# The low halves of the projection weights computed on VectorE instead of GpSimd

## The chip, the cores and the metric

The kernel runs on one core of one Trainium2 chip. A core has TensorE (PE, with its weight loads shown as PEld), VectorE (DVE), ScalarE (ACT), GpSimd (POOL) and SyncE (SP, which here only sends DMAs). Each takes its own instructions strictly in order. The metric is the time of one execution on the device in microseconds; of several runs the median is given.

## The reference

One layer of a hybrid decoder on 512 tokens of width 2048, in fp32:

```
xn   = rmsnorm(h, attn_norm_g)
proj = xn @ w_in                       # 2048 x 7184: columns of both head groups
o_a  = hgrn2(a_q, a_f, a_i)            # 8 heads, S_t = diag(f_t) S_{t-1} + (1-f_t) v_t
o_b  = gated_delta(l2norm(conv(q)), l2norm(conv(k)), conv(v), beta, g)   # 8 heads
h    = h + concat(gated_rmsnorm(o_a), gated_rmsnorm(o_b)) @ w_out
hn   = rmsnorm(h, ffn_norm_g)
qry  = hn @ w_query                    # 8 heads x 2 halves x 128
s1, s2 = qry[..., :128] . sub_keys[0], qry[..., 128:] . sub_keys[1]
best, pos = top16(top16(s1) + top16(s2)); gate = softmax(best)
h    = h + sum_e gate_e * gelu(hn . u_e) * v_e       # 16384 experts, 128 picked a token
out  = rmsnorm(h, final_norm_g)
```

## The kernel before, in words

**Two halves of a weight.** Every large product is made of three matmuls in a reduced fp32 format (fp32r). A weight block of 128 x 1024 (`wunit`, line 94) is loaded by SP into `wr`; ACT copies it to `wh` in that format (line 100, the high half); a subtraction `wl = wr - wh` makes the low half (line 102). The activations are split alike (`xh`, `xl`, later `yh`, `yl`, and `mh`, `ml` for the mixed heads). PE then adds `wh*xh + wh*xl + wl*xh` for each of the block's eight 128 x 128 pieces (`mm3`, lines 239 to 241; `linear`, lines 113 to 115; `scores`, lines 946 to 950, where the raw `wr` is used as well). The three tiles `wr`, `wh`, `wl` have three buffers each.

**Which engine subtracts.** `wunit` takes an engine. The expert tables (`u_steps`, `v_chunk`) ask for DVE: 512 blocks. The three projections do not, and get POOL: 114 blocks of the input projection, 32 of the output projection, 32 of the query projection, 178 in all.

**Stages.** (1) Prologue: load x, split it, sum its squares. POOL squares eight of the sixteen slices (line 774), DVE adds them up (line 776), and the sum gives the norm. (2) Four gated-delta pairs, each a chain of small steps: decays, keys, a block inverse by forward substitution on DVE (lines 498 and 500, 31 steps), a detour through DRAM (gNd, gTd), the rest of the inverse on PE (lines 527, 533, 542), then a recurrence over four chunks (lines 557 to 576). Between these steps the stream of input projections runs on PE: each step of the chain lets it go forward by a given rate (`run`, 1.8 pieces a step for the pairs, 5 for the HGRN heads). A finished projection goes through a causal convolution on DVE (lines 362 and 364) or a gate. Line 380 is the sum of squares for q's and k's norm. (3) Eight HGRN heads, first step line 614. (4) Output projection. (5) PEER scores: for each of 16 n a product, its scaling by the norm on DVE (`t_y`, line 956), four small score products (line 959) and top-16 steps on DVE; after each second n the sums `cd` (line 977) and their top-16. (6) All 16384 experts for 352 tokens, and the picked ones for 160 tokens by gathered rows.

**What sets the order.** The program is written as generators that yield to each other, and a scheduler then places each engine's instructions by a cost model and by the readiness of their inputs and buffers. The order on each engine is fixed when the program is built. So the engine of one instruction also moves others.

The lines that the change touches and what calls them:

Of the kernel before, what the change touches and what calls it, by code (L numbers as in the profile page):

```python
# [14 lines left out]
F32 = mybir.dt.float32  # L15
# [6 lines left out]
ALU = mybir.AluOpType  # L22
# [55 lines left out]
class Kernel:  # L78
# [12 lines left out]
        return (pool or self.fp).tile(list(shape), dt, tag=tag, name=self.nm(tag), bufs=bufs)  # L91


    def wunit(self, src, raw=False, eng=None):
        nc, wp = self.nc, self.wp
        full = raw
        raw = wp.tile([P, 8, P], F32, tag="wr", name=self.nm("wr"))
        nc.sync.dma_start(raw, src)
        hi = wp.tile([P, 8, P], F32R, tag="wh", name=self.nm("wh"))
        nc.scalar.copy(hi, raw)  # L100
        lo = wp.tile([P, 8, P], F32R, tag="wl", name=self.nm("wl"))
        (eng or nc.gpsimd).tensor_tensor(lo, raw, hi.bitcast(F32), op=ALU.subtract)  # L102
        return (raw, hi, lo) if full else (hi, lo)

    def linear(self, src, halves, xh, xl, ps):
# [1001 lines left out]
    def u_steps(self, et):  # L1107

        nc = self.nc
        ps = self.pt("lin")[:, 0:TD]  # L1110
        for h in (0, 1):
            hi, lo = self.wunit(self.a["u"][et][h], eng=nc.vector)
            for k in range(8):
                self.mm3(ps, hi[:, k], lo[:, k], 8 * h + k, k + h == 0, 8 * h + k == KT - 1)
            if h == 0:
                yield
        hid = self.ft("hid", (P, TD), bufs=2, pool=self.dp)
        nc.vector.tensor_tensor(hid, ps, self.r[:, 0:TD], op=ALU.mult)
        nc.scalar.activation(hid, hid, AF.Gelu)
        yield  # L1120
        yield hid
# [29 lines left out]
    def v_chunk(self, g, dc, w, last):  # L1151

        nc = self.nc
        wh, wl = w
        hi, lo = self.wunit(self.a["v"][g, dc].rearrange("p (x y) -> p x y", x=8), eng=nc.vector)
        hv, lv = (x.rearrange("p (e z) n -> p e (z n)", e=4) for x in (hi, lo))
        for dd in range(2):
            dt = 2 * dc + dd
            sl = slice(dd * P, (dd + 1) * P)
            ps = self.pt(self.vtags[self.vn % len(self.vtags)])[:, 0:TD]  # L1160
            self.vn += 1
            for e in range(4):
                nc.tensor.matmul(ps, hv[:, e, sl], wh[:, e], start=(e == 0), stop=False)  # L1163
                nc.tensor.matmul(ps, hv[:, e, sl], wl[:, e], start=False, stop=False)  # L1164
                nc.tensor.matmul(ps, lv[:, e, sl], wh[:, e], start=False, stop=(e == 3))  # L1165
            nc.vector.tensor_tensor(self.hT[:, dt], self.hT[:, dt], ps, op=ALU.add)
            if last:
                if dt == 0:
                    self.acc = self.ft("t_acc", (P, TD), pool=self.fop)
                self.square_sum(self.acc, [(self.hT[:, dt], slice(0, TD))], dt == 0, nc.vector)  # L1170
                nc.scalar.activation(self.hT[:, dt], self.hT[:, dt], AF.Copy, scale=self.g_fin[:, dt:dt + 1])
# [174 lines left out]
```

## Time and profile before

| | |
|---|---|
| three runs, median | 3533.93 us (3527.35 to 3548.31) |
| profiled execution, its own time | 3537.38 us |
| its span, first to last instruction | 3534.2 us |
| busy: PE, PEld, DVE, ACT, POOL | 94%, 87%, 78%, 34%, 25% of the span |
| mean granted clock of PE | 0.966 |
| POOL's subtractions (line 102) | 178, 432.8 us, starting from 6.8 to 1336.5 us |
| DVE's subtractions (line 102) | 512, 623.3 us, starting from 1347.2 us on |

Times are in microseconds; "x52" is a count of instructions. A row of a group gives line, engine, operation, out<-in, shapes and count, then busy time and the mean length of one in ns, then the idle time of the engine just before these instructions and what ended it. A row in order of time gives start, length, engine, line and, in brackets, a wait before it and what ended that. In a table of stretches each engine's busy time stands with its count, then PE's granted clock, the DMA engines' share and the rate in GB/s. Matmuls are pipelined: the length of one is more than its share of PE's time.

### The profile page before, as it was taken

To read this page: it belongs to the slowest core of one execution; us is meant where nothing else is said; L and a number is where in the kernel's file an instruction comes from. 1 tells how busy PE (TensorE), PEld (TensorE's weight loads), DVE (VectorE), ACT (ScalarE), POOL (GpSimd) and SP (SyncE) were. 2 spreads that over 40 slices of the span, in tenths; PEclk is the share of its full clock that TensorE was granted. 3 is DMA by queue.
4 is the path that set the end of the run, shared out by engine and by line. 5 is a ranking of instruction groups with operands and counts; after the bars stand their busy time and mean duration, and the time that the engine had idled before them with its cause. 6 is when DMAs were issued, how large, how long until landed. Compare 5 with 4: busy or idle time off the path is not lost.

```text
span 3534.2 us, 49832 instructions
## 1 busy us (share of the span) xinstructions
PE 3323.9 (94%) x19740; PEld 3085.3 (87%) x19740; DVE 2760.3 (78%) x4095; ACT 1206.8 (34%) x1499; POOL 878.8 (25%) x533
## 2 busy tenths in 40 slices
PE   7889899999999997898999799999999998999997
PEld 5667678888788896898989799999999998999997
DVE  7675654444534679998999799998999998999966
ACT  5333433322332212343435233332333334333334
POOL 4232223333354231011121222222222222111100
PEclk9899989999999998999999999999999999999999
DMA  4232222222442223677788899999999999999963
GB/s 147 76 96 88 83 64 81 78 81 78 130 130 85 71 66 120 209 293 292 277 318 294 316 346 375 370 368 355 358 360 365 372 366 333 349 322 335 332 183 111
DMA packets 238028, 801.63 MB, mean 227 GB/s; under 512 B 30202, under 2 KB 99066, under 8 KB 194978
## 3 DMA queue, kind: packets, MB, share of 16 engines
q1 hardware_dynamic: 191714, 462.88, 37.9%
q0 software_dynamic: 46080, 335.56, 25.2%
q8 instruction: 154, 2.52, 0.3%
q14 instruction: 80, 0.66, 0.1%
HBM read 754.50 MB, written 43.86 MB: 226 GB/s over the span
## 4 chain that ended last, share of the span: by engine, by line
PE 51%; DVE 19%; issue 14%; DMA 12%; POOL 2%; ACT 1%; SPq 0%; DVEq 0%; POOLq 0%; ACTq 0%
PE lin L239 8%; PE lin L241 7%; PE lin L240 7%; DMA row<-vn,eidx 3%; DVE wl L102 3%; DMA wr<-u 3%; PE g L1165 2%; PE g L1164 2%; PE g L1163 2%; POOL row L1205 2%; PE lin L1165 2%; PE lin L1164 2%; PE lin L1163 2%; DVE row L1218 2%; DMA wr<-v 1%
## 5 line engine op out<-in xcount | busy, mean ns | idle before, releaser
L100 ACT CAST wh<-wr 128x1024 fp32r<-128x1024 f32 x690 | 724.5, 1050 | 1708.8 <-DMA wr<-v 402.3
L241 PE MATMUL lin<-yh,wl 128*128 128x352 f32 x2048 | 673.0, 329 | 68.5 <-DVE wl L102 68.2
L102 DVE TENSOR_TENSOR wl<-wr,wh 128x1024 fp32r<-128x1024 f32 x512 | 623.3, 1219 | 81.6 <-ACT wh L100 80.3
L239 PE MATMUL lin<-yh,wh 128*128 128x352 f32 x2048 | 673.3, 329 | 9.5 <-ACT wh L100 9.5
L240 PE MATMUL lin<-yl,wh 128*128 128x352 f32 x2048 | 668.0, 326 | 0.0
L102 POOL TENSOR_TENSOR wl<-wr,wh 128x1024 fp32r<-128x1024 f32 x178 | 432.8, 2432 | 872.8 <-ACT wh L100 809.8
L241 PEld LDWEIGHTS lin<-yh,wl 128*128 128x128 f32 x2048 | 391.3, 191 | 78.8 <-DVE wl L102 78.4
L1205 POOL DMA_INDIRECT row<-un,eidx x160 | 212.4, 1328 | 809.7 <-DVE row L1218 626.2
L239 PEld LDWEIGHTS lin<-yh,wh 128*128 128x128 f32 x2048 | 391.7, 191 | 11.3 <-ACT wh L100 11.3
L1205 POOL DMA_INDIRECT row<-vn,eidx x160 | 201.2, 1258 | 782.8 <-DVE y_nat L1231 416.0
L240 PEld LDWEIGHTS lin<-yl,wh 128*128 128x128 f32 x2048 | 391.1, 191 | 0.0
L239 PE MATMUL lin<-xh,wh 128*128 128x512 f32 x912 | 381.4, 418 | 8.9 <-ACT xh L766 8.8
L1165 PE MATMUL g<-wgh,wl 128*128 128x352 f32 x1188 | 384.9, 324 | 3.5 <-DVE wl L102 3.3
L1164 PE MATMUL g<-wgl,wh 128*128 128x352 f32 x1188 | 385.4, 324 | 0.0
L1163 PE MATMUL g<-wgh,wh 128*128 128x352 f32 x1188 | 382.4, 322 | 2.3 <-ACT wh L100 2.3
L240 PE MATMUL lin<-xl,wh 128*128 128x512 f32 x912 | 375.5, 412 | 2.5 <-DVE xl L767 2.3
L241 PE MATMUL lin<-xh,wl 128*128 128x512 f32 x912 | 373.0, 409 | 4.4 <-POOL wl L102 4.4
L1231 DVE SCALAR_TENSOR_TENSOR y_nat<-row,ww,y_nat 128x2048 f32<-128x2048 f32 x128 | 300.3, 2346 | 11.1 <-DMA row<-vn,eidx 10.7
L1218 DVE SCALAR_TENSOR_TENSOR row<-row,hn_nat 128x2048 f32<-128x2048 f32 x128 | 292.1, 2284 | 1.7 <-DMA row<-un,eidx 1.5
L1165 PEld LDWEIGHTS g<-wgh,wl 128*128 128x128 f32 x1188 | 223.3, 188 | 5.5 <-DVE wl L102 5.4
L1163 PEld LDWEIGHTS g<-wgh,wh 128*128 128x128 f32 x1188 | 223.5, 188 | 2.6 <-ACT wh L100 2.6
L1164 PEld LDWEIGHTS g<-wgl,wh 128*128 128x128 f32 x1188 | 223.2, 188 | 0.0
(348 smaller groups left out, 5879.5 us busy)
## 6 DMA issues: line engine op xcount, KB each, us to landing
wr<-u SPq DMA_DIRECT2D x256, 512.0 KB, 6.2
wr<-v SPq DMA_DIRECT2D x256, 512.0 KB, 6.7
wr<-wi SPq DMA_DIRECT2D x114, 512.0 KB, 3.6
gd<-st SPq DMA_DIRECT2D x11, 2048.0 KB, 13.6
gm<-gd SPq DMA_DIRECT2D x32, 704.0 KB, 9.3
wr<-wo SPq DMA_DIRECT2D x32, 512.0 KB, 3.6
wr<-wq SPq DMA_DIRECT2D x32, 512.0 KB, 3.5
hidd<-hid SPq DMA_DIRECT2D x64, 176.0 KB, 5.2
```

Source lines behind the costliest of these rows:

```text
L100: nc.scalar.copy(hi, raw)
L102: (eng or nc.gpsimd).tensor_tensor(lo, raw, hi.bitcast(F32), op=ALU.subtract)
L239: mm(ps, hi, self.xh[:, k], start=first, stop=False)
L240: mm(ps, hi, self.xl[:, k], start=False, stop=False)
L241: mm(ps, lo, self.xh[:, k], start=False, stop=last)
L1163: nc.tensor.matmul(ps, hv[:, e, sl], wh[:, e], start=(e == 0), stop=False)
L1164: nc.tensor.matmul(ps, hv[:, e, sl], wl[:, e], start=False, stop=False)
L1165: nc.tensor.matmul(ps, lv[:, e, sl], wh[:, e], start=False, stop=(e == 3))
L1205: ins = nc.gpsimd.indirect_dma_start(out=r, out_offset=None, in_=self.a[tab], in_offset=bass.IndirectOffsetOnAxis(ap=idx, axis=0))
L1218: nc.vector.scalar_tensor_tensor(r, r, 1.0, hn, op0=ALU.mult, op1=ALU.mult, accum_out=ww[:, i:i + 1])
L1231: nc.vector.scalar_tensor_tensor(y, r, ww[:, i:i + 1], y, op0=ALU.mult, op1=ALU.add)
```

## The change

`wunit` loses its engine argument and always subtracts on DVE. The calls that named DVE drop the argument. Nothing else is edited; POOL keeps the eight squares of the prologue, a memset, small scalings in the output projection, a copy, five of the final products, and all gathers.

```diff
-    def wunit(self, src, raw=False, eng=None):
+    def wunit(self, src, raw=False):
...
         hi = wp.tile([P, 8, P], F32R, tag="wh", name=self.nm("wh"))
         nc.scalar.copy(hi, raw)
         lo = wp.tile([P, 8, P], F32R, tag="wl", name=self.nm("wl"))
-        (eng or nc.gpsimd).tensor_tensor(lo, raw, hi.bitcast(F32), op=ALU.subtract)
+        nc.vector.tensor_tensor(lo, raw, hi.bitcast(F32), op=ALU.subtract)
...
-            hi, lo = self.wunit(self.a["u"][et][h], eng=nc.vector)
+            hi, lo = self.wunit(self.a["u"][et][h])
...
-        hi, lo = self.wunit(self.a["v"][g, dc].rearrange("p (x y) -> p x y", x=8), eng=nc.vector)
+        hi, lo = self.wunit(self.a["v"][g, dc].rearrange("p (x y) -> p x y", x=8))
```

The scheduler orders the first five stages anew; from the end of the scores on, every engine has the same order as before. Three places show it. The names carry running numbers that are the same in both programs.

On PE, at the first step of the inverse of the first pair (L527; `lin` is the projection that runs beside it), before:

```order
L240 MATMUL lin_1049<-xl,wh_1098 128x512
L241 MATMUL lin_1049<-xh,wl_1100 128x512
L239 MATMUL lin_1049<-xh,wh_1098 128x512
L527 MATMUL g_814<-fc,gT 32x32 x8
L240 MATMUL lin_1049<-xl,wh_1098 128x512
L241 MATMUL lin_1049<-xh,wl_1100 128x512
```

and now:

```order
L239 MATMUL lin_1179<-xh,wh_1235 128x512
L240 MATMUL lin_1179<-xl,wh_1235 128x512
L527 MATMUL g_814<-fc,gT 32x32 x8
L241 MATMUL lin_1179<-xh,wl_1237 128x512
L239 MATMUL lin_1179<-xh,wh_1235 128x512
```

The same step of the chain has the next projection beside it: 416 projection matmuls stand ahead of it instead of 364. At the first step of the first HGRN head (L614) it is 1512 instead of 1423; at the second head's the counts are 1586 and 1584, and from there on equal.

On DVE, near the end of the first pair's substitution (L498, L500), before:

```order
L498 TENSOR_TENSOR t_sq_721<-iN_531,iT_532 128x8x6
L500 TENSOR_TENSOR iT_532<-iT_532,t_sq_721 128x8x6
L498 TENSOR_TENSOR t_sq_724<-iN_531,iT_532 128x8x5
L500 TENSOR_TENSOR iT_532<-iT_532,t_sq_724 128x8x5
L498 TENSOR_TENSOR t_sq_727<-iN_531,iT_532 128x8x4
```

and now:

```order
L498 TENSOR_TENSOR t_sq_721<-iN_531,iT_532 128x8x6
L444 TENSOR_TENSOR geg_389<-gq_507,geg_389 128x512
L500 TENSOR_TENSOR iT_532<-iT_532,t_sq_721 128x8x6
L444 TENSOR_TENSOR geg_410<-gq_507,geg_410 128x512
L498 TENSOR_TENSOR t_sq_724<-iN_531,iT_532 128x8x5
L102 TENSOR_TENSOR wl_1237<-wr_1233,wh_1235 128x1024
L500 TENSOR_TENSOR iT_532<-iT_532,t_sq_724 128x8x5
```

A subtraction stands between two steps of the substitution, and q's scaling (L444) has come forward.

On DVE, in the scores, around the scaling of a product whose predecessor closes a pair of n (L956), now:

```order
L968 MATCH_REPLACE c_1457_8661<-best,cd_8660 128x256
L956 TENSOR_TENSOR t_y_8745<-lin_8668,rstd 128x512
L969 MAX best<-c_1457_8661 128x8
L102 TENSOR_TENSOR wl_8778<-wr_8774,wh_8776 128x1024
L970 MAX_INDEX pos<-best,c_1457_8661 128x8
L966 MAX v_8076<-g_8747 128x8
L102 TENSOR_TENSOR wl_8816<-wr_8812,wh_8814 128x1024
```

Before, these rows stood there without the two subtractions. On PE nine matmuls of the next product (lin_8773) came ahead of the score products of this one (L959) before; now two do, because the third reads wl_8778:

```order
L946 MATMUL lin_8773<-yh,wh_8776 128x352
L947 MATMUL lin_8773<-yl,wh_8776 128x352
L959 MATMUL g_8747<-skt,t_y_8745 128x128 x4
L948 MATMUL lin_8773<-yh,wl_8778 128x352
L950 MATMUL lin_8773<-xg,wr_8774 128x160
```

On SP, the write of the first pair's substitution (gTd, L504) stands behind two more weight loads than before (wr_1378 and wr_1442), and its reading back (gT, L508) behind two more as well (wr_1442 and wr_1472).

## The prediction

> **What bounds the kernel now.** I read the page first (engines, slices; the granted clock is the one slice row that matters below), then busy time by stage, then who waits for whom in the stages that the change touches, then the rows in order of time on VectorE (DVE) and GpSimd (POOL).
>
> ```profile
> PEclk9899989999999998999999999999999999999999
> ```
>
> Not one engine bounds this kernel from end to end, so I cut it at its stages: prologue, gated-delta pairs, HGRN heads, output projection, PEER scores, and the expert part.
>
> ```profile
> core 0: us, PE busy (x) PEld busy (x) DVE busy (x) ACT busy (x) POOL busy (x), PEclk, DMA share, GB/s
> 0.00:60.00 60.00, 39.39 (x127) 27.47 (x127) 48.66 (x62) 32.84 (x45) 33.26 (x21) 0.91 0.47 170
> 60.00:514.00 454.00, 404.44 (x2058) 315.96 (x2058) 287.63 (x579) 171.62 (x236) 127.71 (x52) 0.87 0.28 84
> 514.00:930.00 416.00, 412.66 (x2252) 342.45 (x2251) 191.60 (x363) 122.07 (x145) 137.52 (x58) 1.00 0.25 78
> 930.00:1113.00 183.00, 178.36 (x795) 146.31 (x795) 71.35 (x84) 65.02 (x101) 87.83 (x47) 1.00 0.41 127
> 1113.00:1353.00 240.00, 223.97 (x1457) 219.34 (x1455) 165.41 (x760) 43.23 (x50) 72.93 (x32) 0.97 0.24 75
> 1353.00:3534.00 2181.00, 2065.05 (x13060) 2033.79 (x13058) 1995.65 (x2250) 772.05 (x924) 419.57 (x325) 0.98 0.85 311
> ```
>
> After 1353 us the subtraction is already on DVE and the order of every engine is the same in both kernels; those 2181 us I leave alone. The HGRN heads and the output projection keep TensorE (PE) busy 99% and 97% of the time at full clock with DVE under half: PE sets their length, and no term comes from them. What can move lies in the prologue, the pairs and the scores.
>
> How much is in the pairs? One full stretch gives the price of a 512-wide projection matmul, and one row per stage gives their number (one of three equal lines).
>
> ```profile
> 1000.00:1100.00 100.00, 100.00 (x443) 82.81 (x442) 33.86 (x36) 29.23 (x46) 52.04 (x28) 1.00 0.30 96
> 60.00:514.00 454.00, 172.49 (x408) 81.85 (x408) 0.87 0.28 84
> 514.00:930.00 416.00, 190.15 (x464) 87.30 (x464) 1.00 0.25 78
> ```
>
> 100/443 is 0.226 us a matmul. The HGRN stage has 3 x 464 = 1392 of them, 314 us; its other 860 matmuls have at most 416 - 314 = 102 us, 0.12 us each. By these prices the pairs' 1224 + 834 matmuls need at most 277 + 100 = 377 of their 454 us. So at least 77 us of PE time there go to waits and to the lower clock (0.87), about 19 us for each of the four pairs. The longest named wait:
>
> ```profile
> PE g L380 <- ACT t_sq L376: 30.2, 4, 9.1
> PE g L959 <- DVE t_y L956: 15.8, 7, 2.4
> ```
>
> The first row is the pairs', the second the scores'. Both waits end with DVE work, so DVE's delays count in these two stages.
>
> **The change part by part.** 178 subtractions leave POOL and come to DVE (114 units of the input projection, 32 of the output projection, 32 of the query projection).
>
> ```profile
> L102 DVE TENSOR_TENSOR wl<-wr,wh 128x1024 fp32r<-128x1024 f32 x512 | 623.3, 1219 | 81.6 <-ACT wh L100 80.3
> L102 POOL TENSOR_TENSOR wl<-wr,wh 128x1024 fp32r<-128x1024 f32 x178 | 432.8, 2432 | 872.8 <-ACT wh L100 809.8
> ```
>
> That is 178 x 1.219 = 217 us more on DVE and 433 us less on POOL. It would be a plain loss for DVE if POOL's subtractions cost DVE nothing now. They do cost it:
>
> ```profile
> 216.25 2.38 POOL L102 TENSOR_TENSOR wl<-wr,wh 128x1024 fp32r<-128x1024 f32 x1 [3.05 <-ACT wh L100]
> 216.33 2.56 DVE L498 TENSOR_TENSOR t_sq<-iN,iT 128x224 f32<-128x224 f32 x1
> 218.92 0.39 DVE L500 TENSOR_TENSOR iT<-iT,t_sq 128x224 f32<-128x224 f32 x1
> ```
>
> A 0.39 us multiply that starts 0.08 us after a POOL subtraction ends 0.26 us after it: it stood still. In the pairs this shows in group means.
>
> ```profile
> L500 DVE TENSOR_TENSOR iT<-iT,t_sq 128x248 f32<-128x248 f32 (+30 forms) x124 | 57.0, 459 | 3.5
> L498 DVE TENSOR_TENSOR t_sq<-iN,iT 128x248 f32<-128x248 f32 (+30 forms) x124 | 48.8, 394 | 6.0 <-PE g L380 2.2 <-DMA iN<-gNd 0.5
> L364 DVE SCALAR_TENSOR_TENSOR t_y<-pad,sm,t_y 128x512 f32<-128x512 f32 x45 | 45.6, 1013 | 0.8
> L362 DVE TENSOR_SCALAR t_y<-pad,sm 128x512 f32<-128x512 f32 x15 | 14.8, 984 | 0.2
> 214.12 0.42 DVE L500 TENSOR_TENSOR iT<-iT,t_sq 128x248 f32<-128x248 f32 x1
> 250.18 0.18 DVE L500 TENSOR_TENSOR iT<-iT,t_sq 128x8 f32<-128x8 f32 x1
> 227.25 0.75 DVE L364 SCALAR_TENSOR_TENSOR t_y<-pad,sm,t_y 128x512 f32<-128x512 f32 x1
> 226.61 0.48 DVE L362 TENSOR_SCALAR t_y<-pad,sm 128x512 f32<-128x512 f32 x1
> ```
>
> Undisturbed, L500 falls evenly from 0.42 to 0.18 us, mean 0.30, and L498 reads alike. The excess is 124 x 0.16 + 124 x 0.09 + 45 x 0.26 + 15 x 0.50 = 20 + 11 + 12 + 8 = 51 us on 166 us of work. The other 121 us of DVE in the stage may hold none of it or the same share, 37 us: 51 to 88 in all. Against that stand 52 x 1.219 = 63 us of new subtractions. **Pairs, DVE's own load:** between 25 less and 12 more; I take 0, since what is hit by POOL and what will stand behind a subtraction are the same kind of work.
>
> [...]
>
> **Pairs, order.** Now POOL's time no longer enters the order, and the projections come forward: at the first inverse step of the first pair (L527) 416 projection matmuls stand ahead of it on PE instead of 364, at the end of the pairs (first L614) 1512 instead of 1423, and from the second HGRN head on the counts are equal. So 89 matmuls, 89 x 0.226 = 20 us of PE work, move from a stage that PE fills into one with at least 77 us to spare. They must not lengthen the pairs: the largest insertion is 52 matmuls, 11.8 us, against 19 us spare per pair. The ends are 0 (each insertion delays its pair by as much; SP's write of gTd also stands behind two more weight loads) and 20. I take 16, nearer to 20 by that comparison. With q's projection earlier, the L380 wait should shrink first.
>
> **Prologue.** The sums that lead to the first norm are hit hardest.
>
> ```profile
> 33.49 11.61 DVE L776 TENSOR_TENSOR t_acc<-t_acc,t_sq 128x512 f32<-128x512 f32 x7
> 36.24 8.32 POOL L102 TENSOR_TENSOR wl<-wr,wh 128x1024 fp32r<-128x1024 f32 x3
> 23.44 0.68 DVE L776 TENSOR_TENSOR t_acc<-t_acc,t_sq 128x512 f32<-128x512 f32 x1
> ```
>
> Seven additions at 0.68 would take 4.8, so 6.8 us are lost; the three subtractions now stand behind the last sum, where DVE waits 3 us for the norm anyway. But three earlier ones (3.7 us) come ahead of it and POOL's squares stay. Between 8 less and 0; I take 4 less.
>
> **Scores.** A period of two n takes 30.3 us.
>
> ```profile
> 1174.91 0.69 DVE L956 TENSOR_TENSOR t_y<-lin,rstd 128x512 f32<-128x512 f32 x1 [7.61 <-PE lin L950]
> 1181.34 0.99 DVE L977 TENSOR_TENSOR cd<-v 128x256 f32<-128x256 f32 x1
> 1183.83 0.41 DVE L977 TENSOR_TENSOR cd<-v 128x256 f32<-128x256 f32 x1
> 1188.17 1.30 DVE L977 TENSOR_TENSOR cd<-v 128x256 f32<-128x256 f32 x1
> 1191.23 0.67 DVE L956 TENSOR_TENSOR t_y<-lin,rstd 128x512 f32<-128x512 f32 x1
> 1191.96 1.16 PE L959 MATMUL g<-skt,t_y 128*128 128x128 f32 x8 [2.21 <-DVE t_y L956]
> 1205.17 0.69 DVE L956 TENSOR_TENSOR t_y<-lin,rstd 128x512 f32<-128x512 f32 x1 [6.79 <-PE lin L950]
> ```
>
> From 1174.91 to 1191.23 DVE works without a gap, two of the four cd sums stretched by 0.89 and 0.58, and PE then waits 2.2 us. No subtraction is ordered into that piece, so it shortens by 1.5. Behind it the next unit's subtraction waits for t_y and one MAX8 and takes 1.22; the third matmul of the next group needs it, and PE now reaches L959 with two matmuls of that group done instead of nine: about 0.6 lost. The other two subtractions lie where DVE waits 6.8 to 7.6 us for PE. 0.9 x 7 periods: 6 less (10 less to 4 more, if the early matmuls are lost without return).
>
> **Sum:** 0 - 16 - 4 - 6 = -26. On the profiled execution (span 3534.2, its time 3537.4) that is 3508 and 3511; the median of the runs shown, 3533.9, is at the span, and from it I forecast 3508 us. The first DVE waits that come next are those of the new subtractions on ScalarE's copy (wh).
>
> **The rivals.** *The clock comes back too.* A projection matmul lasts 424 ns in the pairs where undisturbed it lasts 389:
>
> ```profile
> L241 PE MATMUL lin<-xh,wl 128*128 128x512 f32 x408 | 173.2, 424 | 0.0
> L115 PE MATMUL lin<-mh,wl x224: 389/389/389, 961.7 to 1113.3; 128*128 128x512 f32 x112
> ```
>
> If the fuller PE keeps its clock, 1224 x 0.035 = 43 us more go: 3465. For it: 0.87 in the pairs against 1.00 in the stages without gaps. Against it: the inverse and the chain of states stay serial. [...]
>
> *Hidden anyway.* The pairs keep their length and the insertions delay the chains: only prologue and scores remain, -10: 3524, no change that can be told. For it: SP's queue sends loads and the chain's own DMAs in one order, and more loads now stand ahead of the latter.
>
> *Slower: DVE stands in line behind ScalarE's copy.* On POOL a subtraction waited 4.5 us (809.8/178) for wh and blocked nobody; on DVE the chain's next multiply, copy or t_y is queued behind it, and PE behind that. In the pairs the copy itself waits:
>
> ```profile
> ACT wh L100 <- issue: 55.7, 19, 8.1
> ACT wh L100 <- PE lin L240: 31.4, 10, 4.4
> ```
>
> At 87.1/52 = 1.7 us for each this costs 87 us; at what DVE's 512 subtractions pay now (81.6/512 = 0.16) it costs 8. It decides from 26/52 = 0.5 us. In the middle, 0.6 us, 31 us are lost and the insertions win nothing: -10 + 31, 3555 us.
>
> **How the numbers follow.** Forecast 0.47 (its own range 3494 to 3522), clock 0.18, hidden 0.22, slower 0.13. About 0.5%, 18 us, is what a measurement here can tell from no change. Faster than 3516: most of the first, all of the second: 0.60. Within: 0.27. Slower than 3551: 0.13. The range runs from just under the clock's case to past the hidden one, 3462 to 3540.
>
> **What would show it.** Right: L498 and L500 means near 0.30, seven t_acc additions near 5 us, 52 to 63 subtractions on DVE in the pairs, the L380 wait well under 30, the HGRN heads starting with the same end of the pairs or earlier and about 15 us shorter; the scores' period near 29.4. Wrong: DVE idle for wh above 30 us before 514, or the pairs longer by as much as the heads are shorter. If the long DVE rows stay without POOL's subtractions, the first step is false.

## The result

The changed kernel takes **3443.78 us** (median of 4 runs, 3431.63 to 3449.55) against 3533.80 for the kernel before (4 runs, 3527.35 to 3548.31): a ratio of 0.9745, 95% interval 0.9713 to 0.9778. That is 90 us less; the forecast was 26 less, in a range of 3462 to 3540. The direction was right and the size was not. The profiled execution took 3449.55 us, its span is 3447.8.

The same table of stretches as before, for the changed kernel, cut at the same instructions:

```profile
core 0: us, PE busy (x) PEld busy (x) DVE busy (x) ACT busy (x) POOL busy (x), PEclk, DMA share, GB/s
0.00:51.00 51.00, 35.08 (x126) 25.61 (x127) 42.44 (x66) 31.02 (x43) 12.76 (x13) 0.93 0.56 199
51.00:450.00 399.00, 392.39 (x2151) 313.99 (x2150) 279.52 (x637) 174.05 (x240) 0.00 (x0) 0.96 0.35 101
450.00:833.00 383.00, 382.56 (x2092) 318.75 (x2092) 204.90 (x402) 115.68 (x139) 0.00 (x0) 0.99 0.25 77
833.00:1025.00 192.00, 190.31 (x868) 155.32 (x867) 88.12 (x132) 68.24 (x105) 22.14 (x15) 1.00 0.41 126
1025.00:1270.00 245.00, 228.09 (x1452) 222.08 (x1450) 184.88 (x790) 43.31 (x50) 2.47 (x2) 0.96 0.24 74
1270.00:3447.00 2177.00, 2064.09 (x13060) 2034.15 (x13058) 1995.01 (x2250) 773.16 (x924) 412.92 (x325) 0.98 0.85 312
```

The second row is the pairs, 399 us where they took 454 before. DVE is busy for 279.5 us there, nearly what it was (287.6), but PE now fills 392.4 of 399 us, and its granted clock is 0.96 instead of 0.87. The last row is the expert part, which was to stay alone and did: 2177 after 2181.

Where the 86 us of span between the two profiled executions went can be read from the starts of instructions that both kernels have: the gates' copy at the end of the prologue (L337), and the first step of each HGRN head (L615, from the first to the last). Before:

```profile
L337 DVE COPY gate_nat<-g x1: 317/317/317, 63.8 to 63.8; 128x160 f32<-128x160 f32 x1
L615 DVE TENSOR_TENSOR gL<-g,fc x8: 691/692/693, 543.9 to 901.4; 128x512 f32<-128x512 f32 x8
```

After:

```profile
L337 DVE COPY gate_nat<-g x1: 317/317/317, 55.0 to 55.0; 128x160 f32<-128x160 f32 x1
L615 DVE TENSOR_TENSOR gL<-g,fc x8: 683/692/693, 479.7 to 816.2; 128x512 f32<-128x512 f32 x8
```

The prologue gives 8.8 us, the stretch from the gates to the first head 55.4 (480.1 to 424.7), and the heads 21.0 (357.5 to 336.5), nearly all of it in the first head, which has 89 projection matmuls less beside it. That is 85.2 of the 86.4. The rest is small: the scores are 6 us longer, the other stages some us shorter.

The groups of the pairs, after:

```profile
L241 PE MATMUL lin<-xh,wl 128*128 128x512 f32 x439 | 176.5, 402 | 0.0
L102 DVE TENSOR_TENSOR wl<-wr,wh 128x1024 fp32r<-128x1024 f32 x56 | 68.3, 1220 | 22.3 <-ACT wh L100 22.1
L498 DVE TENSOR_TENSOR t_sq<-iN,iT 128x248 f32<-128x248 f32 (+30 forms) x124 | 36.1, 291 | 3.3
L500 DVE TENSOR_TENSOR iT<-iT,t_sq 128x248 f32<-128x248 f32 (+30 forms) x124 | 36.0, 290 | 3.2
L364 DVE SCALAR_TENSOR_TENSOR t_y<-pad,sm,t_y 128x512 f32<-128x512 f32 x45 | 33.5, 745 | 0.3
L362 DVE TENSOR_SCALAR t_y<-pad,sm 128x512 f32<-128x512 f32 x15 | 7.2, 481 | 0.1
L380 PE MATMUL g<-t_sq,fc 128*128 128x512 f32 x16 | 8.6, 619 | 0.8 <-ACT t_sq L376 0.7
```

Every DVE row that was long stands at its undisturbed length: L500 at 290 ns (459 before), L498 at 291 (394), L364 at 745 (1013), L362 at 481 (984). PE's wait for the sum of squares at L380 has gone from 30.2 us to 0.7, and a projection matmul lasts 402 ns instead of 424. The waits of the same stretch show what is late next:

```profile
ACT wh L100 <- PE lin L240: 102.1, 31, 8.1
DVE gT L545 <- PE g L542: 24.1, 8, 9.8
DVE wl L102 <- ACT wh L100: 22.1, 14, 4.8
```

ACT's copy now waits 102 us until PE has read a weight buffer: the weights are ready ahead of PE, and PE itself is what the pairs wait for.

### The profile page after: what moved, and what is told of

Same layout as the page of the kernel before. It is cut to its first block, busy times and chain, and to the rows that moved or that the text cites. A ratio compares the mean times of both kernels' runs of the same rounds, so it can differ in the third digit from the quotient of the medians.

```text
span 3447.8 us, 49787 instructions
## 1 busy us (share of the span) xinstructions
PE 3292.5 (95%) x19740; PEld 3069.9 (89%) x19740; DVE 2794.9 (81%) x4273; ACT 1205.5 (35%) x1497; POOL 450.3 (13%) x355
## 4 chain that ended last, share of the span: by engine, by line
PE 53%; DVE 17%; issue 15%; DMA 10%; POOL 2%; ACT 1%; SPq 0%; DVEq 0%; POOLq 0%; ACTq 0%
PE lin L239 8%; PE lin L241 7%; PE lin L240 7%; DVE wl L102 4%; DMA wr<-u 3%; PE g L1164 3%; PE g L1165 3%; DMA wr<-v 3%; PE g L1163 3%; POOL row L1205 2%; DVE row L1218 2%; PE lin L1164 2%; PE lin L1165 2%; PE lin L1163 2%; DMA row<-vn,eidx 2%
## 5 line engine op out<-in xcount | busy, mean ns | idle before, releaser
L102 DVE TENSOR_TENSOR wl<-wr,wh 128x1024 fp32r<-128x1024 f32 x690 | 840.0, 1219 | 249.7 <-ACT wh L100 241.2
L239 PE MATMUL lin<-xh,wh 128*128 128x512 f32 x912 | 370.3, 406 | 9.1 <-ACT xh L766 8.9
L240 PE MATMUL lin<-xl,wh 128*128 128x512 f32 x912 | 365.9, 401 | 1.4 <-DVE xl L767 1.4
L241 PE MATMUL lin<-xh,wl 128*128 128x512 f32 x912 | 364.2, 400 | 0.3 <-DVE wl L102 0.3
L1205 POOL DMA_INDIRECT row<-un,eidx x160 | 204.9, 1281 | 1041.3 <-DVE row L1218 627.3
L239 PEld LDWEIGHTS lin<-xh,wh 128*128 128x128 f32 x912 | 173.7, 190 | 42.6 <-ACT xh L766 8.9
```

The costliest lines, as they stand in the source:

```text
L102: nc.vector.tensor_tensor(lo, raw, hi.bitcast(F32), op=ALU.subtract)
L239: mm(ps, hi, self.xh[:, k], start=first, stop=False)
L240: mm(ps, hi, self.xl[:, k], start=False, stop=False)
L241: mm(ps, lo, self.xh[:, k], start=False, stop=last)
L1205: ins = nc.gpsimd.indirect_dma_start(out=r, out_offset=None, in_=self.a[tab], in_offset=bass.IndirectOffsetOnAxis(ap=idx, axis=0))
```

## The experiments

The pairs are compared from the gates' copy to the first HGRN head in each kernel's own profile, by one row of the table of stretches each. PE's idle time there is the length less PE's busy time, and since nearly the same matmuls run, more busy time on PE at a lower clock is the clock's share. The two rows to compare with, before:

```profile
64.00:544.00 480.00, 431.17 (x2211) 337.44 (x2210) 295.69 (x601) 184.15 (x254) 132.94 (x54) 0.88 0.28 83
```

and after:

```profile
55.00:480.00 425.00, 418.48 (x2292) 335.82 (x2292) 290.96 (x664) 184.28 (x256) 0.00 (x0) 0.96 0.33 98
```

PE's idle time fell from 48.8 to 6.5 us, 42 less. PE has 81 matmuls more here, 81 x 0.226 = 18 us, and is still busy for 12.7 us less: 31 us are the clock's. -42 - 31 + 18 = -55. These are two causes, and the experiments ask for each. A *hold* below is the time for which an operation on POOL keeps one on DVE from going on; it shows as a longer DVE row (2.56 us for a multiply of 0.39, at 216.33 us before), not as a wait. The diffs are cut to the lines that matter. A profile is one execution, and the clock alone moved the pairs of one and the same order by 11 us (see "Why the clock comes and goes"), so prices taken from one pair of profiles are rough.

### A useless subtraction on POOL as well

```diff
         nc.vector.tensor_tensor(lo, raw, hi.bitcast(F32), op=ALU.subtract)
+        if not (expert or full):
+            nc.gpsimd.tensor_tensor(raw, raw, hi.bitcast(F32), op=ALU.subtract)
```

It runs for the 146 blocks of the input and output projections (the expert tables' calls pass a new argument `expert`, and `full` is true for the query projection); its result is not used. PE's order in the pairs stays within four matmuls of the changed kernel's (416, 769, 1122, 1440 projection matmuls ahead of the four inverses, 1512 at the first head).

> The changed kernel with a second, useless subtraction on GpSimd for each of the 146 blocks of the input and output projections (it writes wr - wh over wr, which nobody reads afterwards; the result stays the reference's). VectorE's work and the order on TensorE stay those of the changed kernel (416, 769, 1122 and 1440 projection matmuls ahead of the four inverses), only GpSimd's hold on VectorE comes back. Theory 'hold' (the pairs got shorter because VectorE no longer stands still during GpSimd's subtractions): the pairs go back to about 450 us or more, the whole to 3500 to 3560. Theory 'order' (they got shorter because the projections come forward): the pairs stay near 400, the whole stays within 3435 to 3460.

3577.93 us (3573.88 to 3581.84), ratio to before 1.0132, interval 1.0110 to 1.0155: 134 us above the changed kernel, 0.92 us for each useless subtraction, more than was expected, and slower than the kernel before; DVE has its own subtraction besides. Its pairs:

```profile
69.00:586.00 517.00, 445.13 (x2290) 352.26 (x2290) 370.64 (x662) 183.06 (x255) 151.47 (x57) 0.87 0.27 80
```

and two of its groups there (the multiplies of the substitution stand two lines lower in this kernel):

```profile
L500 DVE TENSOR_TENSOR t_sq<-iN,iT 128x248 f32<-128x248 f32 (+30 forms) x124 | 56.6, 457 | 3.7 <-PE g L382 0.6
L502 DVE TENSOR_TENSOR iT<-iT,t_sq 128x248 f32<-128x248 f32 (+30 forms) x124 | 56.3, 454 | 3.2
```

They are as long as before, and 92 us of the 134 are lost in the pairs: PE idles 71.9 us there and its clock is back at 0.87. PE's largest wait is back as well, with the changed kernel's order (30.2 us before, 0.7 after; the line numbers are two higher):

```profile
PE g L382 <- ACT t_sq L378: 43.3, 4, 12.0
```

DVE's rows grew by 79.7 us (291.0 to 370.6), so one microsecond by which POOL stretched a DVE row cost 92/79.7 = 1.15 us of the stage. That POOL's subtraction stops DVE is shown; its price in this pair of profiles is a little more than one to one.

### Which work of POOL stops DVE

```diff
+        if not (expert or full):
+            nc.gpsimd.memset(raw, 0.0)
+            nc.gpsimd.memset(raw, 1.0)
```

Two fills for each of the 146 blocks, of a buffer whose content is no longer needed; they write and read nothing.

> Control of the first: instead of the useless subtraction GpSimd writes constants over wr, twice (about 1.9 us each block, 146 blocks), reading nothing from SBUF. If any work of GpSimd holds VectorE, the pairs lengthen as with the subtraction, in proportion (1.9 to 2.4): 3490 to 3540. If only an operation that reads does, or if the hold is not the cause at all: 3440 to 3455.

3451.37 us (3441.05 to 3459.60), ratio 0.9785, interval 0.9761 to 0.9810. In the pairs:

```profile
L104 POOL MEMSET wr<- 128x1024 f32 x57 | 54.7, 959 | 306.1 <-DVE wl L102 266.3 <-ACT wh L100 15.4 <-ACT t_sq L295 13.5
L105 POOL MEMSET wr<- 128x1024 f32 x57 | 54.6, 957 | 3.3
L501 DVE TENSOR_TENSOR t_sq<-iN,iT 128x248 f32<-128x248 f32 (+30 forms) x124 | 36.1, 291 | 3.2
L365 DVE TENSOR_SCALAR t_y<-pad,sm 128x512 f32<-128x512 f32 x15 | 7.9, 524 | 0.1
L460 DVE TENSOR_SCALAR gN<-gkN,gate_g 128x128 f32<-128x128 f32 x32 | 8.0, 368 | 6.9 <-PE g L536 6.9
```

109 us of POOL's writing leave the multiplies at 291 ns. What became longer are scalings with one tensor as input: the convolution's from 481 to 524 ns, where a single one of 15 took 1111 ns, and the one of `gN` from 280 to 368. So it is not that POOL is busy; the subtraction, beside which the multiplies took 457 and 454 ns, also reads. The fills also keep the weight buffer much as the useless subtraction does (109/57 = 1.9 us a block against 151.5/57 = 2.7), so that a buffer comes free later is not what the subtraction costs. Why the scalings grew is not shown.

### Shorter holds

```diff
+            nc.gpsimd.tensor_tensor(raw[:, 0:4], raw[:, 0:4], hi.bitcast(F32)[:, 0:4], op=ALU.subtract)
```

The useless subtraction at half the width.

> The changed kernel with a useless POOL subtraction of half the width (128x512, about 1.2 us) for each of the 146 blocks of the input and output projections; output unchanged. Full width cost 134 us. If the cost goes with the time that POOL holds DVE: half, 67 us, 3511. If there is slack that short holds fit into (as DVE's idle time suggests): under 40 us, 3445 to 3484. If each hold costs alike whatever its length: 3578.

3496.21 us (3491.07 to 3504.35), ratio 0.9920, interval 0.9887 to 0.9953.

```profile
60.00:518.00 458.00, 427.58 (x2291) 340.02 (x2291) 328.72 (x663) 183.43 (x255) 88.50 (x57) 0.93 0.30 91
```

52 us above the changed kernel by the medians, 62 by the two ratios (0.0175 x 3534): 39% to 46% of 134, between the two expectations and nearer the first. Such a hold took 1.55 us in the pairs (88.5/57) where the full width took 2.66 (151.5/57). DVE's rows grew by 37.8 us and the pairs by 33, 0.87 each. So the cost grows with the time that POOL holds; whether short holds find a little slack, the two prices (0.87 and 1.15) are too rough to say.

### The same load on DVE itself

```diff
+            nc.vector.tensor_tensor(raw, raw, hi.bitcast(F32), op=ALU.subtract)
```

A second, useless subtraction on DVE for the same 146 blocks. The scheduler puts somewhat more projections ahead of the first three inverses (471, 866, 1226, 1440).

> The changed kernel with a second, useless subtraction on DVE for each of the 146 blocks of the input and output projections (1.22 us each, 178 us in all, about 78 of them before the first HGRN head); output unchanged. Theory (what counts is where the time falls: a subtraction in DVE's own order stands at a place that the order chose, a hold by POOL falls anywhere and is twice as long): at most 20 us, 3444 to 3465. Rival (every us that DVE cannot work costs alike; useless POOL subtractions of 2.43 us cost 0.92 us each, so 1.22 us on DVE cost 0.46): 67 us, 3511.

3495.72 us (3493.06 to 3507.07), ratio 0.9897, interval 0.9843 to 0.9950: 52 us above the changed kernel. My theory gave 20 at most and falls; the rival's 67 is nearer.

```profile
57.00:524.00 467.00, 433.75 (x2295) 345.77 (x2294) 354.85 (x724) 187.81 (x258) 0.00 (x0) 0.92 0.30 91
```

DVE has 63.9 us more to do in the pairs, and these are 42 longer: 0.66 us for each. So DVE's time is not free there, though 0.66 is not its price alone: the order differs, and 12.5 of the 42 us are one wait of the fourth inverse for its way through DRAM. But the first subtraction was nearly so, which another profile shows (the next but one below): with the subtractions (68 us of them) on DVE the pairs took 414 us for 406.0 us of PE work, so at most 8 us of PE's idle time can be laid to anything on DVE. The first 68 us fit in beside PE, the second 64 mostly don't.

### The order alone

```diff
-RATE_B, RATE_A, OWED = 1.8, 5.0, 6.0
+RATE_B, RATE_A, OWED = 2.4, 5.0, 6.0
```

The kernel before, with more projections let into the pairs: 363, 764, 1083, 1388 ahead of the inverses and 1485 at the first head (before 364, 682, 1004, 1323 and 1423).

> The kernel before with one number changed: 2.4 instead of 1.8 projection pieces for each step of a pair's chain. GpSimd subtracts as before, the projections come forward on TensorE: 363, 764, 1083, 1388 matmuls ahead of the four inverses and 1485 ahead of the first HGRN head (before 364, 682, 1004, 1323, 1423; changed kernel 416, 765, 1125, 1437, 1512). Theory 'order': most of the gain comes, 3460 to 3485. Theory 'hold': at most the work moved, (1485 - 1423) x 0.226 = 14 us: 3515 to 3535.

3531.96 us (3526.49 to 3541.82), ratio 0.9994, interval 0.9977 to 1.0011: nothing.

```profile
65.00:549.00 484.00, 432.51 (x2273) 340.75 (x2272) 303.56 (x604) 189.20 (x259) 139.59 (x56) 0.91 0.29 85
```

62 matmuls more, 14 us, made the pairs 4 us longer, and the heads, which had that work less, came 3 us earlier at the second one (591.6 to 588.8). At the end nothing is left of it. While POOL holds DVE, filling PE's idle time by the order alone wins nothing here. The opposite corner, the old order without the holds, was not run.

### The pairs alone put back, and all but them

The subtractions of blocks 9 to 64, those of the pairs, back on POOL (`wn` counts the blocks from 0):

```diff
-        nc.vector.tensor_tensor(lo, raw, hi.bitcast(F32), op=ALU.subtract)
+        self.wn += 1
+        eng = nc.gpsimd if 8 < self.wn <= 64 else nc.vector
+        eng.tensor_tensor(lo, raw, hi.bitcast(F32), op=ALU.subtract)
```

> The changed kernel, with the 56 subtractions that run during the pairs (blocks 9 to 64 of the input projection) back on POOL; all others stay on DVE. Theory (POOL's subtractions hold DVE up inside the chains of the pairs): the pairs are as long again as in the kernel before, only the prologue's 9 us stay, 3515 to 3530. Rival (the gain of 55 us came from somewhere else, POOL's absence in the other stages or DVE's share of work there): 3440 to 3470.

3493.35 us (3482.39 to 3507.21), ratio 0.9882, interval 0.9826 to 0.9938. Neither theory: 50 us of the gain are lost, 40 are kept, and the prologue explains 9 of these.

```profile
55.00:504.00 449.00, 398.24 (x2202) 313.12 (x2201) 301.72 (x602) 183.51 (x254) 133.32 (x54) 0.95 0.29 88
```

```profile
PE g L383 <- ACT t_sq L379: 35.8, 4, 9.8
```

PE's idle time is back at 50.8 us (48.8 before), and its largest wait with it (30.2 before). PE's order is nearly that of the kernel before again (380, 702, 1028, 1326 projection matmuls ahead of the inverses), so this run alone does not part the holds from the order; the useless subtraction, with the order kept, does. But PE's busy time is 33 us less than before for nine matmuls less, and the clock is 0.95 where it was 0.88; the whole kernel's clock was 0.975 to 0.977 in its four executions, like the changed kernel's (0.976 to 0.980), against 0.963 to 0.972 in those of the kernel before. So the two causes can be had apart: the idle time belongs to POOL's subtractions in the pairs, while most of the clock came back without moving them.

The complement: blocks 65 to 178 (heads, output projection, query projection) on POOL, prologue and pairs on DVE (the same edit with `64 < self.wn <= 178`).

> The complement: the first 64 blocks' subtractions (prologue and pairs) stay on DVE, the other 114 (HGRN heads, output projection, query projection) go back to POOL. Theory: nothing is lost, since PE sets the length of the heads and of the output projection whatever DVE does, and the scores get their 5 us back as with the query projection alone: 3436 to 3446. Rival (holds cost outside the pairs too, at the 0.92 us that each cost with useless subtractions): 82 blocks of heads and output projection cost 75 us, 3515.

3456.33 us (3442.23 to 3459.51), ratio 0.9791, interval 0.9737 to 0.9844, not to be told from the changed kernel, whose ratio lies in this interval, though the median is above the 3436 to 3446 expected. The rival's 3515 is out (the interval ends at 0.9844 x 3533 = 3478): outside prologue and pairs POOL's holds cost 13 us by the medians and nothing that is clear of the noise. Its pairs, whose 2286 matmuls have the changed kernel's order, are the profile that was referred to above:

```profile
55.00:469.00 414.00, 406.02 (x2286) 325.45 (x2285) 291.36 (x661) 183.50 (x255) 2.46 (x1) 0.99 0.34 100
```

### The prologue alone, and all but it

`8 < self.wn <= 178` on POOL leaves only the prologue's eight subtractions on DVE; PE's order in the pairs is that of the kernel with the pairs put back.

> Only the first 8 blocks' subtractions (the prologue) on DVE, the other 170 on POOL as before; on PE the pairs have the same order as in the kernel with the pairs' 56 on POOL (380, 702, 1028, 1326 projection matmuls ahead of the four inverses, where the kernel before has 364, 682, 1004, 1323). Question: that kernel kept 30 us of the pairs' gain, and its granted clock, with POOL's holds in the pairs. If the prologue's change (its 9 us and the 16 to 24 matmuls more ahead of each inverse) brings the clock: the same here, less the 5 us of the scores, 3485 to 3495. If DVE's subtractions after the pairs brought it: only the prologue's 9 us are left, 3520 to 3530.

3505.43 us (median of 10 runs, 3496.81 to 3515.85) beside 3527.32 for the kernel before in the same comparison, ratio 0.9944, interval 0.9923 to 0.9965: 20 us less, between the two expectations.

```profile
54.00:511.00 457.00, 406.37 (x2207) 319.54 (x2207) 300.70 (x603) 184.27 (x255) 133.92 (x54) 0.93 0.29 87
```

PE idles for 50.6 us, as with the pairs put back, and the clock lies between: 0.93.

The counterpart, `self.wn <= 8` on POOL:

> The counterpart: the first 8 blocks' subtractions on POOL, the other 170 on DVE as in the changed kernel (413, 765, 1125, 1437 projection matmuls ahead of the inverses, the changed kernel has 416, 765, 1125, 1437). If the prologue only gives its own 9 us: 3450 to 3457. If it decides the clock of the pairs too: about 30 us more, 3475 to 3490.

3461.41 us (3456.28 to 3470.75), ratio 0.9819, interval 0.9781 to 0.9857.

```profile
63.00:491.00 428.00, 420.54 (x2300) 336.35 (x2300) 291.06 (x662) 184.19 (x255) 0.00 (x0) 0.96 0.33 98
```

The prologue is 8.3 us longer again and the pairs are nearly those of the changed kernel (428 us after 425). The median is 18 us above the changed kernel's, more than the 6 to 13 expected; of the 21 us between the two profiled executions 10 lie behind the last scaling of the scores (2187.8 us to the end after 2177.6), where the order is the same, so part of it is noise. The two halves add up: 0.56% and 1.81% make 2.37%, the whole change is 2.55%.

### Why the clock comes and goes

Just ahead of three of the four inverses of the kernel before, PE pauses for the substitution's way through DRAM (1.6, 3.1 and 1.8 us). Around the first inverse, before, the table of stretches shows the pause, what follows, and the recovery:

```profile
134.90:138.30 3.40, 1.91 (x28) 1.44 (x28) 0.69 (x1) 1.51 (x3) 2.18 (x1) 1.00 0.35 71
138.30:158.80 20.50, 20.50 (x128) 15.29 (x129) 4.60 (x14) 3.92 (x7) 2.54 (x2) 0.50 0.14 44
158.80:169.00 10.20, 10.20 (x61) 8.10 (x61) 4.12 (x13) 2.19 (x5) 1.30 (x1) 1.00 0.11 35
```

For 20.5 us PE is busy without a gap at half clock and does 128 matmuls. The changed kernel has the same:

```profile
123.40:126.90 3.50, 2.44 (x30) 1.65 (x29) 0.34 (x1) 0.36 (x1) 0.00 (x0) 0.99 0.74 200
126.90:147.30 20.40, 20.40 (x128) 15.54 (x128) 6.10 (x15) 3.47 (x7) 0.00 (x0) 0.50 0.10 29
```

but a kernel that differs from it only long after this place (the query projection on POOL, below) has not:

```profile
121.80:125.20 3.40, 2.31 (x28) 1.41 (x27) 1.00 (x1) 0.36 (x1) 0.00 (x0) 1.00 0.80 176
125.20:145.70 20.50, 20.50 (x184) 15.80 (x181) 9.64 (x23) 5.39 (x11) 0.00 (x0) 1.00 0.12 38
```

The same pause (PE idle for 1.06 of 3.50 us, and for 1.09 of 3.40), once followed by half clock and 128 matmuls, once by full clock and 184. So with the same order the clock fell in one execution and not in the other: by the granted clock the pairs of the changed kernel lost 0.04 of 425 us and those of that kernel 0.01 of 414, a difference of 13 us, which covers the 11 by which the two stages differ.

The pauses differ in length from kernel to kernel. PE's waits at the first step of the inverse, in the kernel before and in the one with the pairs put back:

```profile
PE g L527 <- DMA gT<-gTd: 6.5, 3, 3.1
PE g L530 <- DMA gT<-gTd: 3.0, 4, 1.2
```

Before, the three pauses were 1.6, 3.1 and 1.8 us, and half clock came with each, for 20.5, 23.9 and 23.9 us: 68 us, worth 34 at full speed, about the 33 by which PE's busy time is shorter with the pairs put back. With the pairs put back none was longer than 1.2 us, and no stretch at half clock there was longer than 10.2. Over the profiles of all thirteen kernels, each of the twelve pauses of 1.5 us or more at this step came with 20 us or more at half clock, and two of the twelve between 0.75 and 1.4 us did. It is not the only way: some stretches of 17 us and more began inside an inverse without such a pause (17.1 us from 437.5 in the changed kernel). The kernels that still have the holds (0.95 and 0.93) lost less of the clock than the kernel before (0.88), the first of them with pauses of 1.2 us at most where that one had 1.6 to 3.1. Both have 16 to 24 projection matmuls more ahead of each of the first three inverses, which would fill part of the way through DRAM; no run changed that number alone, so it is not shown that it shortens the pauses, nor that the clock follows from it.

### The query projection and the squares

The scores became longer, so the query projection's 32 subtractions went back to POOL:

```diff
-        nc.vector.tensor_tensor(lo, raw, hi.bitcast(F32), op=ALU.subtract)
+        (nc.gpsimd if full else nc.vector).tensor_tensor(lo, raw, hi.bitcast(F32), op=ALU.subtract)
```

> The changed kernel with the 32 subtractions of the query projection back on GpSimd; the 146 of the other two projections stay on VectorE. In the changed kernel the stage of the scores ended 6 us later against the output projection's end than before. Both theories: the pairs stay as in the changed kernel, the scores go back to the old order, and 4 to 8 us go: 3436 to 3440. If the scores' 6 us came from elsewhere: no change against the changed kernel.

3441.18 us (3438.95 to 3445.66), ratio 0.9753, interval 0.9731 to 0.9775. From the first scaling to the last, before:

```profile
1128.00:1353.00 225.00, 208.97 (x1363) 204.93 (x1361) 160.91 (x755) 38.74 (x44) 67.25 (x29) 0.97 0.23 72
```

the changed kernel:

```profile
1039.00:1270.00 231.00, 214.09 (x1363) 208.56 (x1362) 179.92 (x783) 39.27 (x44) 0.00 (x0) 0.96 0.23 70
```

and with the query projection on POOL:

```profile
1027.70:1253.60 225.90, 210.50 (x1361) 206.66 (x1361) 160.91 (x755) 39.04 (x43) 67.88 (x29) 0.96 0.23 72
```

The 6 us are the query projection's; in the total they are lost among the runs. With the eight squares of the prologue on ACT besides:

```diff
-                if k % 2:
-                    nc.scalar.activation(sq, x[:, k], AF.Square)
-                else:
-                    nc.gpsimd.tensor_tensor(sq, x[:, k], x[:, k], op=ALU.mult)
+                nc.scalar.activation(sq, x[:, k], AF.Square)
```

> The changed kernel with the query projection's 32 subtractions on POOL and the eight squares of the prologue that POOL makes on ACT instead: nothing of POOL that reads SBUF is left ahead of the norm. If the squares still stretch DVE's additions, the norm's sum starts up to 5 us earlier and the total is 3432 to 3440; if ACT, which then makes all sixteen, is late instead, 3441 to 3450.

3439.79 us (3436.56 to 3454.82), ratio 0.9755, interval 0.9698 to 0.9812. The prologue ends 5 to 6 us earlier (the gates' copy at 49.2, after 54.0 with the squares on POOL and 55.0 in the changed kernel), which the total doesn't show with certainty. No variant beats the changed kernel by more than the measurement can tell.

## Why the prediction was right or wrong

**What bounds the kernel.** Right, and it held the answer. It found at least 77 us of PE time in the pairs that went to waits and to the lower clock. The way from the gates to the end of the heads became 55.4 + 21.0 = 76 us shorter. That the two numbers meet is partly luck: 77 was a lower bound, and the pairs of one order took 414 or 425 us. The prediction then gave only 16 of the 77 a way out. Its first row of waits names ACT's square, not DVE work; that DVE stood behind it the row does not show, but ACT's own waits do (11.9 us for the substitution, 4.4 for a scaling).

**Pairs, DVE's own load: this is the step that failed.** The text took 0 "since what is hit by POOL and what will stand behind a subtraction are the same kind of work". As a sum over DVE's time it was right: 295.7 us busy before and 291.0 after, and the stretch estimated at 51 to 88 us is 295.7 - (291.0 - 69.5) = 74 (57 subtractions, 69.5 us, lie in this stretch). As a price it was wrong. A stretch lies inside the multiplies and convolutions on which the chain waits. Where holds were added, it cost 0.87 to 1.15 us of the stage for each microsecond. Where they were taken out of the pairs alone (from the kernel with the pairs put back to the changed one), it was worth 0.55: the stage became 24 us shorter with 90 matmuls, 20 us, more in it, for 301.7 - (291.0 - 69.5) = 80 us of stretch. The first subtraction of each block, on DVE, goes where the order finds room and cost at most 8 us in all. So 74 us of stretch were worth 41 to 85, and what came in their place 8 at most. The term should have been about -33 to -85 for the pairs at equal PE work; measured at equal PE work, -55 - 18 = -73. Of the 73, 42 are PE's idle time, which adding the holds brought back and taking them out removed. The other 31 are the clock's, and these are not owed to the holds alone: with the holds the pairs' clock was anywhere from 0.87 to 0.95.

**Pairs, order (-16).** The lead itself appeared: the heads are 21 us shorter, and the forecast's "about 15 us shorter" was close. But it isn't a gain of the order alone. The kernel before with a like order gained nothing. The 18 us of moved work had to be paid for in the pairs, and the room for it came from the holds' end, not from the 77 us that were idle with the holds in place. The comparison of the largest insertion with "19 us spare per pair" took the spare time for usable; it was time in which the chain was late. What the order adds once the holds are gone is open, since no run had the old order without them.

**Prologue (-4, ends -8 and 0).** -9. The splits of x and the fourteen additions, before:

```profile
L767 DVE SCALAR_TENSOR_TENSOR xl<-x_in,sm,xh 128x512 fp32r<-128x512 f32 x16 | 18.7, 1223 | 4.4 <-ACT xh L766 4.4
L776 DVE TENSOR_TENSOR t_acc<-t_acc,t_sq 128x512 f32<-128x512 f32 x14 | 18.3, 1356 | 0.0
```

and after:

```profile
L767 DVE SCALAR_TENSOR_TENSOR xl<-x_in,sm,xh 128x512 fp32r<-128x512 f32 x16 | 15.1, 993 | 0.8 <-ACT xh L766 0.8
L776 DVE TENSOR_TENSOR t_acc<-t_acc,t_sq 128x512 f32<-128x512 f32 x14 | 10.6, 799 | 0.0
```

Of the additions' excess, 14 x (1.36 - 0.68) = 9.5 us, 7.7 came back; with the squares on ACT as well (above) they took 684 ns each, so the rest was the squares'. The three subtractions ahead of the norm cost 3.6 us, as the text said (3.7). What it left out are the splits of x (L767): they were stretched too and won those 3.6 us back.

**Scores (-6, ends -10 and +4).** +6, the wrong sign and outside its ends. The `cd` sums shrank as the text said, yet PE's wait for the scaled product did not. The changed kernel's row beside the 15.8 us quoted in the prediction:

```profile
PE g L959 <- DVE t_y L956: 14.9, 8, 2.1
```

The text counted the matmuls that no longer stand ahead of that wait as 0.6 us lost per period. They cost more; that PE had next to nothing left to do in the wait is argued, not shown. PE is idle for 16 us before and 17 after, and busy for 5 us longer at the same count of matmuls (214.1 against 209.0 us). The granted clock, 0.96 after 0.97, accounts for about half of these 5 us; the rest is open.

**The rivals.** "The clock comes back too" was right about the clock: 31 of the 86 us are the clock's, its price was 43, and its condition, a fuller PE, came true (392.4 of 399 us). That the fuller PE is what raised the clock is not shown: with the pairs put back PE idled for 50.8 us and the clock was 0.95. It put the time at 3465 because it stood on the forecast's other terms; the idle time was missing from both. "Hidden anyway" and "slower" are out: DVE waited 22.1 us for ACT's copy in the pairs, 0.4 us for each subtraction and below the 0.5 from which that rival was to decide, and while DVE waited PE had work.

**What would show it.** The means near 0.30 us, 56 subtractions in the pairs, the L380 wait under 30 and the shorter heads came as listed. The additions of the prologue (799 ns where 680 was undisturbed) nearly did, and the scores' period, (1270 - 1039)/7.5 = 30.8 instead of 29.4, did not.

## What to carry to other kernels

A microsecond that one engine steals inside the operations of a serial chain isn't worth a microsecond of work that the scheduler may place: price the first near the chain's rate (here 0.55 to 1.15 us of the stage for each), and the second only at what no longer fits beside the engine that bounds the stage (here at most 8 us for 68 us of subtractions). When a stage holds a large sum of idle time and lowered clock (here 77 us) and its chain is being stretched, forecast from that sum downward, not from the rows' balance upward. And an order that fills idle time can be worth nothing, as it was here (62 matmuls more, ratio 0.9994), as long as what made the time idle stays.

## What the runs showed of the hardware

Of the two kinds of work tried on POOL in the pairs, only the one that reads made DVE's two-input operations longer: 109 us of fills left them at 291 ns, while 151 us of subtractions made them 455. The subtractions' cost at the end grew with the time held: 134 us with holds of 2.66 us in the pairs, 52 to 62 with holds of 1.55. One-input scalings were longer beside the fills (481 to 524 ns, 280 to 368).

After a pause of about a microsecond (1.06 us at the first inverse of the changed kernel) PE's clock was at half for 20.4 us, although PE was busy without a gap throughout: 128 matmuls, where a kernel with the same order, PE idle for 1.09 us there, did 184 in 20.5 at full clock. At the first step of the inverse over the thirteen profiles, 12 of 12 pauses of 1.5 us and more came with such a drop, and 2 of 12 from 0.75 to 1.4. At PE's longest wait in the kernel before, 9.1 us for ACT's square, no matmul ran from 355.9 to 365.0; the clock was at half from 360.2 to 370.4, the last 5.4 us of it with PE busy. So the longer wait came with the shorter stretch at half clock, 10.2 us against 20.5 to 23.9 at the inverses of the same kernel. What makes this difference, no run here shows.
